# Turned queries and first keys emptied from PSUM for both heads at once, their halves laid out by transfers on ScalarE's queue

## The chip, the cores and the metric

The program runs on one core of a Trainium2 chip, in one launch. The metric is device time in microseconds, lower is better. One core has TensorE (PE, matmul; it writes to PSUM, and only VectorE and ScalarE read PSUM here), VectorE (DVE), ScalarE (ACT), GpSimd (POOL) and SyncE (SP), each with an instruction queue of its own that is worked off in order. Transfers are issued from the queues of SP, ACT or POOL and are moved by 16 DMA engines.

## The reference

Two layers; each is a SwiGLU feed-forward half step, a mixer, and another feed-forward half step, over 512 positions of width 1024 in fp32. The change lies in the mixer:

```python
def hybrid_mixer(h, ...):
    proj = h @ w_in
    qa, ka, va, ub, qc, kc, vc, f_lin, g_lin = jnp.split(proj, SPLIT_POINTS, axis=-1)
    ya = chunked_relpos_attention(ha(qa), ha(ka), ha(va), qk_gain[0], qk_gain[1], rel_bias)
    yb = multiscale_pool(ub, w_pool, pool_scale)
    yc = forgetting_attention(hc(qc), hc(kc), hc(vc), qk_gain[2], qk_gain[3], f_lin + forget_bias)
    ys = jnp.stack([ya, yb, yc], axis=2)
    branch = jnp.einsum('bsnw,nwd->bsnd', ys, w_branch)
    gates = jax.nn.sigmoid(g_lin.reshape(B, S, N_BRANCHES, D_MODEL))
    return jnp.sum(gates * branch, axis=2) @ w_out
```

Both attentions have 8 heads of width 64. Queries and keys are RMS-normalised per head and multiplied by a gain (`rms_norm(q, gq) * dh ** -0.5`), logits are `q . k` plus a bias (the first) or a difference of summed forget gates (the second), masked, then softmax and the product with the values.

## The kernel before, in words

**Numbers in two parts.** Every fp32 operand is split into a high part (fp32r) and a low part, the rest, and a product is three matmuls: high x high, high x low, low x high (`triple`, lines L140 to L142 for projections with 512 columns). A weight chunk `raw` is loaded by SP (L303), its high part is made by a cast on ACT (L312) and its low part by a subtraction on DVE (L314).

**The mixer.** `run` projects the first attention's queries (column 0), its keys (1), the forget gates and its values (2), one behind the other. Then come the 8 heads of the first attention ("a"), and between its steps, as filler, the projections of the second attention's queries (column 3), keys (4) and values (5). The second attention ("c") follows. `attention` goes over heads and, in a head, over four blocks of 128 queries. One step is `logits` (two matmuls: for odd and even heads the high and the low part of the query against a key tile that holds high and low), DVE adds the bias and takes the maximum (L1154), ACT takes the exponential (L1158), DVE the reciprocal of the sum (L1160), GpSimd scales (L1162; DVE for the last block). Some units later the weights are transposed on TensorE (L1174), taken out of PSUM in two parts by ACT (L1178) and DVE (L1179), and multiplied with the values (L1196, L1197); ACT and DVE take the result out (L1200 to L1202). After each step the filler yields projections until a budget of TensorE units is used.

**Queries and keys.** `proj_qk` copies a projection out of PSUM (L1001), squares it (ACT L1003), sums the squares (DVE L1004), and forms and applies the norms (DVE, L1022). `turn(p)`, once for each pair of heads (p from 0 to 3), transposes 128 columns (4 instructions, L1027) into a PSUM tile `pt` of 128 x 512: the even head's 64 numbers in the upper 64 partitions, the odd head's in the lower. It then fills tiles `b` of 128 x 2 x 512. A key tile holds, for each head, the high part on the head's own partitions and the low part on the other ones. A query of the version before has two tiles: the high part on both halves (ACT writes the own half at L1036, a transfer on GpSimd's queue copies it to the other, L1039), and the low part on the own half (DVE, L1042) with zeros on the other (GpSimd, L1040). ACT and DVE do this for the even head, then for the odd one.

**Order of the work.** The PSUM pool behind `mmt()` has four banks; turns, logits, weights' transposes and products with the values share it. Tiles `b` come from a pool of 17, tiles `v2` from one of 4. The order in which work is written out is set by a clock `pe[0]` that counts estimated TensorE time: `later(delay, fn)` gives a task a due time, and `poll()`, called in every product, runs the tasks that are due. `ready(p)` is due `TURN` (52) units and 12 per pair behind the end of a projection, 12 more for the first keys, and waits for a head of the attention to be reached (`Q_GATE`, `K_GATE`). A list scheduler then sets each engine's order. The tile names of the order shown below carry a running number.

Of the kernel before, what the change touches and what calls it, by code (L numbers as in the profile page):

```python
# [15 lines left out]
F32 = mybir.dt.float32  # L16
F32R = mybir.dt.float32r
I32 = mybir.dt.int32
AF = mybir.ActivationFunctionType
ALU = mybir.AluOpType  # L20
AX = mybir.AxisListType

P = 128
# [17 lines left out]
def encoder_kernel(tc, xT, c, w_ada, b_ada, gains, w_gate, w_up, w_down, w_qkv, w_f, w_ubg,  # L41
                   qk_gain, rel, fbias, w_pool, pool_scale, w_branch, w_out, inv_cnt, w_first, out):
    nc = tc.nc
# [12 lines left out]
    mm = nc.tensor.matmul  # L56
# [7 lines left out]
    def st(shape, dt, tag, bufs):  # L64
        return sb.tile(shape, dt, tag=tag, bufs=bufs, name=nm(tag))
# [25 lines left out]
    def mmt(shape=(P, T)):  # L91
        return ps.tile(list(shape), F32, tag="mm", bufs=4, name=nm("mm"))

    def blk(tag, dt=F32R):
        bufs = {"xv": 4, "v2": 4, "b": NB}[tag]
        return st([P, 2, T], dt, tag, bufs)

    def t1(cols=T):
        return st([P, cols], F32, "t1", 2)

    def t2(cols=T):
        return st([P, cols], F32, "t2", 3)
# [16 lines left out]
    def later(delay, fn, group=None):  # L119
        t = Task(pe[0] + delay, fn, group)  # L120
        tasks.append(t)
        return t
# [197 lines left out]
    def rsqrt_steps(v, n):  # L320

        jt = st([P, n], I32, "nt_j", 2)
        nc.vector.tensor_scalar(jt, v.bitcast(I32), -0.5, 1597463007.0, op0=ALU.mult, op1=ALU.add)
        y = jt.bitcast(F32)
        for _ in range(3):
            yield y
            q = st([P, n], F32, "nt_q", 1)
            u = st([P, n], F32, "nt_u", 1)
            z = st([P, n], F32, "nt_z", 2)
            nc.vector.tensor_tensor(q, y, y, op=ALU.mult)  # L330
            nc.vector.scalar_tensor_tensor(u, q, -0.5, v, op0=ALU.mult, op1=ALU.mult)
            nc.vector.scalar_tensor_tensor(z, u, 1.5, y, op0=ALU.add, op1=ALU.mult)
            y = z
        yield y
# [656 lines left out]
        res.extend(vt)  # L991

    def proj_qk(l, col, gcol, is_q, res, pre=None, norm=None):
        lows = []
        qs = []

        def evac(t, a):
            if t == 0:
                qs.extend((st([P, NT, T], F32, "ptb", 2), st([P, NT, H], F32, "qss", 1)))
            qn, ss = qs  # L1000
            nc.scalar.copy(qn[:, t, :], a)  # L1001
            sq = t2(T)
            nc.scalar.activation(sq, qn[:, t, :], AF.Square)  # L1003
            nc.vector.tensor_reduce(ss[:, t, :], sq.rearrange("p (h d) -> p h d", h=H), axis=AX.X, op=ALU.add)  # L1004

        yield from proj(l, col, evac, pre, norm)
        qn, ss = qs
        norm_of = {}

        def first():  # L1010
            v = st([P, NT * H], F32, "nt_v32", 2)
            nc.vector.tensor_scalar(v, ss.rearrange("p t h -> p (t h)"), 1.0 / HD, EPS, op0=ALU.mult, op1=ALU.add)
            norm_of["steps"] = rsqrt_steps(v, NT * H)
            next(norm_of["steps"])

        def step():
            norm_of["r"] = next(norm_of["steps"])

        def scale(t):
            q3 = qn[:, t, :].rearrange("p (h d) -> p h d", h=H)  # L1020
            r = norm_of["r"][:, t * H:(t + 1) * H].unsqueeze(2).to_broadcast([P, H, HD])
            nc.vector.tensor_tensor(q3, q3, r, op=ALU.mult)  # L1022

        def turn(p):
            pt = mmt()
            for t in range(NT):
                nc.tensor.transpose(pt[:, t * P:(t + 1) * P], qn[:, t, p * P:(p + 1) * P], ident)  # L1027
            pe[0] += 2.2
            b = blk("b")
            if is_q:  # L1030
                lows.append(blk("b"))
            first, second = slice(0, HD), slice(HD, P)
            for odd, (own, other) in enumerate(((first, second), (second, first))):
                dst = b[:, odd, :]
                gc = gcol[own, :]
                nc.scalar.activation(dst[own, :], pt[own, :], AF.Identity, scale=gc)  # L1036
                low = dst[other, :]
                if is_q:
                    nc.gpsimd.dma_start(low.bitcast(F32), dst[own, :].bitcast(F32))  # L1039
                    nc.gpsimd.memset(lows[p][other, odd, :].bitcast(F32), 0.0)  # L1040
                    low = lows[p][own, odd, :]
                nc.vector.scalar_tensor_tensor(low, pt[own, :], gc, dst[own, :].bitcast(F32),  # L1042
                                               op0=ALU.mult, op1=ALU.subtract)
            res.append((b, lows[p]) if is_q else b)

        todo = [first, step, step, step] + [lambda t=t: scale(t) for t in range(NT)]
        todo += [lambda p=p: turn(p) for p in range(4)]
        turns.append(todo)
        for n in range(8):
            later(PACE * n, lambda n=n: todo.pop(0)() if len(todo) == 12 - n else None)  # L1050

        def ready(p):
            if len(todo) >= 4 - p:
                if heads[0] < (Q_GATE if is_q else K_GATE)[p]:
                    later(8, lambda: ready(p))
                else:
                    while len(todo) >= 4 - p:
                        todo.pop(0)()

        for p in range(4):  # L1060
            later(TURN + (12 if col == 1 else 0) + 12 * p, lambda p=p: ready(p))

    turns = []
    heads = [2 * H]
    TURN = 52
# [73 lines left out]
    def attention(qs, ks, vs, strip, ys, filler, budget, group):  # L1139
# [3 lines left out]

        def logits(h, i, strips):
            p, off = divmod(h, 2)
            (q, ql), k = qs[p], ks[p]
            odd = h % 2
            n = (i + 1) * P
            s = mmt()
            mm(s[:, :n], q[:, odd, i * P:(i + 1) * P], k[:, odd, :n], start=True, stop=False)  # L1150
            mm(s[:, :n], ql[:, odd, i * P:(i + 1) * P], k[:, odd, :n], start=False, stop=True)
            lg = t1(T)[:, :n]
            mx = st([P, 1], F32, "mx", 4)
            nc.vector.tensor_tensor_reduce(out=lg, in0=s[:, :n], in1=strips[i], scale=-1.0, scalar=BIG,  # L1154
                                           op0=ALU.add, op1=ALU.min, accum_out=mx)
            pr = t2(T)[:, :n]
            sm = st([P, 1], F32, "sm", 4)
            nc.scalar.activation(pr, lg, AF.Exp, bias=mx, scale=-1.0, accum_out=sm)  # L1158
            rs = st([P, 1], F32, "rs", 4)
            nc.vector.reciprocal(rs, sm)  # L1160
            eng = nc.vector if i == NT - 1 else nc.gpsimd
            eng.tensor_scalar(pr, pr, rs, None, op0=ALU.mult)  # L1162
            pe[0] += 0.5 * (i + 1.5)
            later(LAG_T, lambda: turn(h, i, pr), group)
# [446 lines left out]
```

## Time and profile before

| | |
|---|---|
| median of 3 runs | 2321.46 us (2320.78 to 2321.69) |
| profiled execution | 2320.73 us, span 2318.9 us, TensorE clock 1.0 |
| TensorE (PE) busy | 2296.4 us, 99% of the span |
| VectorE (DVE) busy | 1848.0 us, 80% |
| ScalarE (ACT) busy | 1242.5 us, 54% |
| GpSimd (POOL) busy | 277.1 us, 12% |
| DMA | 325.26 MB, 140 GB/s mean |
| first queries' and keys' turns, first layer | about 398 to 436 us |
| first attention, first layer | from about 437 us; turns of the second attention's queries from 481 us |

The profile shows one execution. "Busy" of an engine is the time in which it had an instruction; "a <- b" in a list of waits says that the engine sat idle before a until b was done. A row of a group gives line, engine, operation, tiles, count, then busy us, mean ns of one, and the idle time of the engine ahead of it with what ended it. A row of a window gives its bounds, its length, the busy time of PE, PEld, DVE, ACT and POOL with their counts, the clock, the DMA share and GB/s. The chain lists, in order of time, the work that ended last. A queue with a q behind it (SPq, ACTq) is the engine's sequencer, which issues transfers.

### The profile page before, as it was taken

The page shows a single profiled execution, that of the slowest core. Times are in us where ns is not written, and L with a number is a line of the kernel's source. Part 1 is how long each engine was busy: PE and PEld are TensorE (multiplying, and loading weights), DVE is VectorE, ACT ScalarE, POOL GpSimd, SP SyncE. Part 2 cuts the span into 40 slices and gives each one's busy share as a digit, 9 for nine tenths or more (in the row PEclk, how much of TensorE's full clock was granted, in tenths as well). Part 3 has the DMA queues.
Part 4 walks back from the last instruction along what each step waited for, and adds up shares of the span by engine and source line. Part 5 has one row for each costly group of instructions (what it writes and reads, how often), then busy time and mean ns, then how long its engine had stood idle before and what let it go on. Part 6 is the DMA issues. An engine that isn't in the chain of part 4 may idle for free.

```text
span 2318.9 us, 38895 instructions
## 1 busy us (share of the span) xinstructions
PE 2296.4 (99%) x14826; PEld 2067.5 (89%) x14826; DVE 1848.0 (80%) x3205; ACT 1242.5 (54%) x2252; POOL 277.1 (12%) x413
## 2 busy tenths in 40 slices
PE   7999999999999999999999999999999999999999
PEld 5898998878889898989999989988788898999898
DVE  8988886787698678888788989777877995859593
ACT  5363555677645463635463636466765554636362
POOL 2000011244400000000000000112443001000000
PEclk9999999999999999999999999999999999999999
DMA  8736353333334526373526372533332445133332
GB/s 300 256 101 243 121 192 99 106 97 116 104 114 146 191 73 218 96 259 101 190 74 218 92 271 93 200 109 101 94 119 94 122 152 172 55 118 97 114 92 100
DMA packets 142174, 325.26 MB, mean 140 GB/s; under 512 B 14338, under 2 KB 16514, under 8 KB 141988
## 3 DMA queue, kind: packets, MB, share of 16 engines
q1 hardware_dynamic: 137426, 307.57, 40.9%
q0 software_dynamic: 4560, 15.21, 2.1%
q8 instruction: 116, 1.90, 0.3%
q14 instruction: 70, 0.57, 0.1%
q10 hardware_dynamic: 2, 0.00, 0.0%
HBM read 312.16 MB, written 6.38 MB: 137 GB/s over the span
## 4 chain that ended last, share of the span: by engine, by line
PE 93%; DVE 3%; ACT 2%; issue 1%; DMA 0%; SPq 0%; POOL 0%; ACTq 0%; DVEq 0%
PE acc L140 13%; PE acc L142 13%; PE acc L141 13%; PE acc L149 7%; PE acc L151 7%; PE acc L150 7%; PE mm L151 5%; PE mm L149 5%; PE mm L150 5%; PE mm L140 5%; PE mm L141 5%; PE mm L142 4%; PE mm L1174 1%; PE mm L1197 1%; PE mm L1196 1%
## 5 line engine op out<-in xcount | busy, mean ns | idle before, releaser
L312 ACT CAST w<-raw 128x1024 fp32r<-128x1024 f32 x205 | 212.8, 1047 | 226.2 <-PE acc L142 142.8
L140 PE MATMUL acc<-b,w 128*128 128x512 f32 (+1 forms) x880 | 326.6, 371 | 0.0
L141 PE MATMUL acc<-b,w 128*128 128x512 f32 (+1 forms) x880 | 323.3, 367 | 0.0
L142 PE MATMUL acc<-b,w 128*128 128x512 f32 (+1 forms) x880 | 323.2, 367 | 0.0
L314 DVE TENSOR_TENSOR w<-raw,w 128x1024 fp32r<-128x1024 f32 x205 | 248.6, 1223 | 88.7 <-ACT w L312 85.1
L142 PEld LDWEIGHTS acc<-b,w 128*128 128x128 f32 x880 | 165.4, 188 | 28.0
L140 PEld LDWEIGHTS acc<-b,w 128*128 128x128 f32 x880 | 165.4, 188 | 26.2
L141 PEld LDWEIGHTS acc<-b,w 128*128 128x128 f32 x880 | 165.4, 188 | 25.9
L149 PE MATMUL acc<-b,ptb 128*128 128x256 f32 x588 | 162.8, 277 | 0.0
L150 PE MATMUL acc<-b,ptb 128*128 128x256 f32 x588 | 162.7, 277 | 0.0
L151 PE MATMUL acc<-b,ptb 128*128 128x256 f32 x588 | 162.6, 277 | 0.0
L140 PE MATMUL acc<-w,hhi 128*128 128x512 f32 x336 | 138.3, 412 | 0.0
L142 PE MATMUL acc<-w,hlo 128*128 128x512 f32 x336 | 131.8, 392 | 0.0
L141 PE MATMUL acc<-w,hhi 128*128 128x512 f32 x336 | 131.7, 392 | 0.0
L565 DVE TENSOR_TENSOR ptb<-pta,ptb 128x1024 fp32r<-128x1024 f32 x70 | 85.7, 1224 | 50.9 <-ACT ptb L564 49.8
L473 DVE SCALAR_TENSOR_TENSOR xv<-acc,badac,xv 128x512 f32<-128x512 f32 (+1 forms) x112 | 77.2, 690 | 58.7 <-PE acc L142 58.7
L149 PE MATMUL mm<-b,ptb 128*128 128x256 f32 x420 | 115.9, 276 | 0.0
L150 PE MATMUL mm<-b,ptb 128*128 128x256 f32 x420 | 115.9, 276 | 0.0
L151 PE MATMUL mm<-b,ptb 128*128 128x256 f32 x420 | 115.9, 276 | 0.0
L565 DVE TENSOR_TENSOR w<-v,w 128x1024 fp32r<-128x1024 f32 x84 | 102.5, 1220 | 16.8 <-ACT w L564 16.8
L226 DVE CUSTOM_DVE_ANT_0 v<-v,b,badac 128x1024 f32<-128x1024 f32 x90 | 113.7, 1278 | 1.9 <-DMA v<-in_w_ada_dram 1.8
L564 ACT CAST w<-v 128x1024 fp32r<-128x1024 f32 x84 | 87.8, 1046 | 42.9 <-PE acc L142 31.5
(346 smaller groups left out, 7368.2 us busy)
## 6 DMA issues: line engine op xcount, KB each, us to landing
v<-in_w_ada_dram SPq DMA_DIRECT2D x106, 512.0 KB, 5.4
raw<-in_w_down_dram SPq DMA_DIRECT2D x88, 512.0 KB, 4.5
raw<-in_w_qkv_dram SPq DMA_DIRECT2D x42, 512.0 KB, 3.6
v<-in_w_gate_dram SPq DMA_DIRECT2D x70, 256.0 KB, 3.5
v<-in_w_up_dram SPq DMA_DIRECT2D x70, 256.0 KB, 3.9
raw<-in_w_gate_dram SPq DMA_DIRECT2D x70, 256.0 KB, 7.2
raw<-in_w_up_dram SPq DMA_DIRECT2D x70, 256.0 KB, 3.4
raw<-in_w_ubg_dram SPq DMA_DIRECT2D x28, 512.0 KB, 3.6
```

The lines of the kernel that those rows point to most:

```text
L140: mm(o, lh, rh, start=start, stop=False)
L141: mm(o, lh, rl, start=False, stop=False)
L142: mm(o, ll, rh, start=False, stop=stop)
L149: mm(o, lh, rh, start=start and k == 0, stop=False, skip_group_check=True)
L150: mm(o, lh, rl, start=False, stop=False, skip_group_check=True)
L151: mm(o, ll, rh, start=False, stop=k == 3, skip_group_check=True)
L226: product = lambda: nc.vector.tensor_tensor_reduce(out=raw, in0=raw, in1=silc[0], scale=1.0, scalar=badac[:, l, j, d:d + 1], op0=ALU.mult, ...
L312: nc.scalar.copy(hi, raw)
L314: lo_eng.tensor_tensor(lo, raw, hi.bitcast(F32), op=ALU.subtract)
L473: nc.vector.scalar_tensor_tensor(x, acc_j, gate, x, op0=ALU.mult, op1=ALU.add)
L564: act_(lambda: nc.scalar.copy(pair[0], src))
L565: vec_(lambda: nc.vector.tensor_tensor(pair[1], src, pair[0].bitcast(F32), op=ALU.subtract))
```

## The change

For the first queries, the first keys and the second queries (columns 0, 1 and 3) a turn takes the whole PSUM tile out with one ACT instruction (high part, both heads, 128 x 512) and one DVE instruction (low part) into a tile `both` of the pool `v2`. Four transfers on ACT's queue lay the halves out. A query pair has now one tile per head, high part on both halves of the partitions in plane 0, low part on both halves in plane 1 (four transfers of 64 x 1024); a key tile keeps its layout (four of 64 x 512). GpSimd's transfers and zeros are gone. The second keys (column 4) keep the old way. The logits' two matmuls read the query's planes 0 and 1. Turns of columns 3 and 4 are due 8 units later.

```diff
             b = blk("b")
-            if is_q:
-                lows.append(blk("b"))
             first, second = slice(0, HD), slice(HD, P)
-            for odd, (own, other) in enumerate(((first, second), (second, first))):
-                dst = b[:, odd, :]
-                gc = gcol[own, :]
-                nc.scalar.activation(dst[own, :], pt[own, :], AF.Identity, scale=gc)
-                low = dst[other, :]
+            if col in (0, 1, 3):
+                both = blk("v2")
+                nc.scalar.activation(both[:, 0, :], pt, AF.Identity, scale=gcol)
+                nc.vector.scalar_tensor_tensor(both[:, 1, :], pt, gcol, both[:, 0, :].bitcast(F32),
+                                               op0=ALU.mult, op1=ALU.subtract)
                 if is_q:
-                    nc.gpsimd.dma_start(low.bitcast(F32), dst[own, :].bitcast(F32))
-                    nc.gpsimd.memset(lows[p][other, odd, :].bitcast(F32), 0.0)
-                    low = lows[p][own, odd, :]
-                nc.vector.scalar_tensor_tensor(low, pt[own, :], gc, dst[own, :].bitcast(F32),
-                                               op0=ALU.mult, op1=ALU.subtract)
-            res.append((b, lows[p]) if is_q else b)
+                    c = blk("b")
+                    moves = [(o[rows], both[own]) for o, own in ((b, first), (c, second)) for rows in (first, second)]
+                else:
+                    moves = [(b[first, 0], both[first, 0]), (b[second, 0], both[first, 1]),
+                             (b[first, 1], both[second, 1]), (b[second, 1], both[second, 0])]
+                for o, part in moves:
+                    nc.scalar.dma_start(o.bitcast(F32), part.bitcast(F32))
+            else:
+                for odd, (own, other) in enumerate(((first, second), (second, first))):
...
+            res.append((b, c) if is_q else b)
...
-            later(TURN + (12 if col == 1 else 0) + 12 * p, lambda p=p: ready(p))
+            later(TURN + (0, 12, 0, 8, 8)[col] + 12 * p, lambda p=p: ready(p))
...
-            (q, ql), k = qs[p], ks[p]
             odd = h % 2
+            q, k = qs[p][odd], ks[p]
...
-            mm(s[:, :n], q[:, odd, i * P:(i + 1) * P], k[:, odd, :n], start=True, stop=False)
-            mm(s[:, :n], ql[:, odd, i * P:(i + 1) * P], k[:, odd, :n], start=False, stop=True)
+            mm(s[:, :n], q[:, 0, i * P:(i + 1) * P], k[:, odd, :n], start=True, stop=False)
+            mm(s[:, :n], q[:, 1, i * P:(i + 1) * P], k[:, odd, :n], start=False, stop=True)
```

Lines of the functions behind it move by some six numbers: the logits are L1150 and L1151 before and L1156 and L1157 now, the exponential L1158 and L1164, the weights' transposes L1174 and L1180, the values' products L1196, L1197 and L1202, L1203; the turn's transposes L1027 and L1026; its ACT instruction L1036 and L1032, its DVE instruction L1042 and L1033, and L1042 is now the transfers.

**What moves on TensorE, at the second attention's queries.** TensorE before, first layer, a little behind the third of these turns; `acc` rows are projections of the second keys (filler), `mm` rows are logits and transposes of the first attention:

```order
L1150 MATMUL mm_5182<-b_4443,b_4195 128x256
L1151 MATMUL mm_5182<-b_4443,b_4196 128x256
L140 MATMUL acc_4864<-w_5160,hhi 128x512
L141 MATMUL acc_4864<-w_5160,hhi 128x512
L142 MATMUL acc_4864<-w_5160,hlo 128x512
L1174 MATMUL mm_5203<-ident,t_851_5083 128x128 x4
L140 MATMUL acc_4865<-w_5155,hhi 128x512
L141 MATMUL acc_4865<-w_5155,hhi 128x512
L142 MATMUL acc_4865<-w_5155,hlo 128x512
```

TensorE now, at the end of the second keys' projection: the rows of `acc_4875` are the end of that filler, and what follows is a product with the values (`mm_5246`) and logits (`mm_5260`), and, behind the rows shown, the fourth query turn and more of attention:

```order
L141 MATMUL acc_4875<-w_5151,hhi 128x512
L142 MATMUL acc_4875<-w_5151,hlo 128x512
L1202 MATMUL mm_5246<-ptb_5124,xv_4413 128x256
L1156 MATMUL mm_5260<-b_4445,b_4193 128x512
L1157 MATMUL mm_5260<-b_4445,b_4193 128x512
L1203 MATMUL mm_5246<-ptb_5124,xv_4413 128x256
L1202 MATMUL mm_5246<-ptb_5124,xv_4456 128x256
L1203 MATMUL mm_5246<-ptb_5124,xv_4456 128x256
L1202 MATMUL mm_5246<-ptb_5124,xv_4486 128x256
L1203 MATMUL mm_5246<-ptb_5124,xv_4486 128x256
L1202 MATMUL mm_5246<-ptb_5124,xv_4508 128x128
```

Before, three to six projections stand between two steps of attention. Now the projections of the second keys stand in long rows (18, then 25 in a row) ahead of this place, and from `mm_5246` on 44 instructions of attention and turns follow without a projection between them; the next projection reads `w_5397`. The longest such row before has 14 instructions.

**On ACT, in the same place.** ACT before, from the first query turn to the third; `w_5372` is the same weight chunk as `w_5397` now:

```order
L1036 ACTIVATE b_5050<-mm_5045,qg_110 64x512 x2
L1200 COPY yl_5072<-mm_5063 64x256
L1036 ACTIVATE b_5094<-mm_5089,qg_110 64x512
L1202 CAST b_4971<-yl_5072 64x256
L1178 CAST pta_5040<-mm_5104 128x2x128
L1158 ACTIVATE t_851_5083,sm_5084<-t_849_5080,mx_5081 128x512
L1036 ACTIVATE b_5094<-mm_5089,qg_110 64x512
L312 CAST w_5372<-raw_5370 128x1024
L1036 ACTIVATE b_5123<-mm_5118,qg_110 64x512
L1178 CAST ptb_5133<-mm_5134 128x3x128
L1158 ACTIVATE t_866_5147,sm_5148<-t_864_5144,mx_5145 128x128
L1200 COPY yl_5171<-mm_5166 64x256
```

ACT now, from the fourth query turn's last transfers to the cast of that chunk:

```order
L1042 DMA b_5281<-v_915_5278 64x1024 x2
L1002 ACTIVATE t_918_5292<-ptb_5202 128x512
L1164 ACTIVATE t_922_5311,sm_5312<-t_920_5308,mx_5309 128x128
L1002 ACTIVATE t_925_5321<-ptb_5202 128x512
L1184 CAST ptb_5324<-mm_5325 128x3x128
L1206 COPY yl_5337<-mm_5332 64x256
L1164 ACTIVATE t_934_5351,sm_5352<-t_932_5348,mx_5349 128x256
L1184 CAST ptb_5324<-mm_5366 128x4x128
L1164 ACTIVATE t_942_5381,sm_5382<-t_940_5378,mx_5379 128x384
L1208 CAST b_5331<-yl_5337 64x256
L1000 COPY ptb_5202<-acc_4875 128x512
L312 CAST w_5397<-raw_5395 128x1024
```

The cast of the next chunk, which stood between the second and the third query turn, now stands behind all four turns and their 16 transfers, and behind the copies and squares of the second keys (L1000, L1002).

**On ACT, at the first keys.** ACT before, from the second key turn (L1036) to the first exponential of attention; `xv` rows are copies of the values out of PSUM (L986):

```order
L1036 ACTIVATE b_4424<-mm_4419,qkgc 64x512
L1036 ACTIVATE b_4443<-mm_4438,qkgc 64x512
L986 CAST xv_4451<-acc_4311 128x4x64
L1036 ACTIVATE b_4443<-mm_4438,qkgc 64x512
L986 CAST xv_4451<-acc_4311 128x4x64
L1036 ACTIVATE b_4467<-mm_4462,qkgc 64x512
L986 CAST xv_4478<-acc_4312 128x4x64
L1036 ACTIVATE b_4467<-mm_4462,qkgc 64x512
L986 CAST xv_4478<-acc_4312 128x4x64
L986 CAST xv_4500<-acc_4313 128x4x64 x2
L1158 ACT_TABLE_LOAD
L1158 ACTIVATE t_685_4514,sm_4515<-t_683_4511,mx_4512 128x128
```

ACT now, from the second key tile's transfers to that exponential:

```order
L1042 DMA b_4423<-v_677_4424 64x512 x4
L1032 ACTIVATE v_680_4446<-mm_4440,qkgc 128x512
L986 CAST xv_4456<-acc_4307 128x4x64
L1042 DMA b_4445<-v_680_4446 64x512 x4
L986 CAST xv_4456<-acc_4307 128x4x64
L1032 ACTIVATE v_684_4473<-mm_4467,qkgc 128x512
L986 CAST xv_4486<-acc_4308 128x4x64
L1042 DMA b_4472<-v_684_4473 64x512 x4
L986 CAST xv_4486<-acc_4308 128x4x64
L986 CAST xv_4508<-acc_4309 128x4x64
L1164 ACT_TABLE_LOAD
L1164 ACTIVATE t_693_4522,sm_4523<-t_691_4519,mx_4520 128x128
```

The four transfers of each key tile stand between the copies of the values, and the table load and the first exponential stand behind the last of them.

More of the change, by code (lines that the diff above doesn't have):

```diff
@@ L993, in proj_qk @@
     def proj_qk(l, col, gcol, is_q, res, pre=None, norm=None):
-        lows = []
         qs = []
@@ L1029, in turn @@
             b = blk("b")
-            if is_q:
-                lows.append(blk("b"))
             first, second = slice(0, HD), slice(HD, P)
-            for odd, (own, other) in enumerate(((first, second), (second, first))):
-                dst = b[:, odd, :]
-                gc = gcol[own, :]
-                nc.scalar.activation(dst[own, :], pt[own, :], AF.Identity, scale=gc)
-                low = dst[other, :]
-                if is_q:
-                    nc.gpsimd.dma_start(low.bitcast(F32), dst[own, :].bitcast(F32))
-                    nc.gpsimd.memset(lows[p][other, odd, :].bitcast(F32), 0.0)
-                    low = lows[p][own, odd, :]
-                nc.vector.scalar_tensor_tensor(low, pt[own, :], gc, dst[own, :].bitcast(F32),
-                                               op0=ALU.mult, op1=ALU.subtract)
-            res.append((b, lows[p]) if is_q else b)
+            if col in (0, 1, 3):
[3 more added lines that the diff above has]
+                                               op0=ALU.mult, op1=ALU.subtract)
+                if is_q:
+                    c = blk("b")
[7 more added lines that the diff above has]
+                for odd, (own, other) in enumerate(((first, second), (second, first))):
+                    dst = b[:, odd, :]
+                    gc = gcol[own, :]
+                    nc.scalar.activation(dst[own, :], pt[own, :], AF.Identity, scale=gc)
+                    nc.vector.scalar_tensor_tensor(dst[other, :], pt[own, :], gc, dst[own, :].bitcast(F32),
+                                                   op0=ALU.mult, op1=ALU.subtract)
+            res.append((b, c) if is_q else b)
         todo = [first, step, step, step] + [lambda t=t: scale(t) for t in range(NT)]
```

## The prediction

> **What bounds the kernel now.** I read the page's busy shares and its chain, then TensorE's list of waits, then the chain, the windows and the timeline of the two attentions, where the change lies.
>
> ```profile
> PE   2296.4 (99%) x14826; PEld 2067.5 (89%) x14826; DVE 1848.0 (80%) x3205; ACT 1242.5 (54%) x2252; POOL 277.1 (12%) x413
> PE 93%; DVE 3%; ACT 2%; issue 1%; DMA 0%; SPq 0%; POOL 0%; ACTq 0%; DVEq 0%
> ```
>
> TensorE is the bound: it is busy in 2296.4 of 2318.9 us. The change adds and removes no matmul, so it can move the time only through TensorE's waits. Those of the mixers are these (us in total, times, longest; both layers):
>
> ```profile
> PE mm L1174 <- DVE b L1042: 2.7, 3, 1.2
> PE mm L1027 <- DVE mx L1154: 1.5, 2, 0.8
> PE mm L1197 <- DVE ptb L1179: 0.7, 2, 0.4
> PE mm L1027 <- DVE ptb L1022: 0.6, 2, 0.3
> PE mm L1196 <- ACT ptb L1178: 0.5, 2, 0.3
> PE mm L1027 <- DVE pta L1179: 0.5, 2, 0.2
> ```
>
> Together 6.5 us, and 5.3 of them (the L1174 row and the three of L1027) stand at a turn or right behind one. That is all a better turn can win. The windows say where: 2.4 us per layer of TensorE's idle time lie in the 38 us in which the second attention's queries are turned (38.00 less 35.61, and less 35.33 in the second layer), none in the 16 us in which the first keys are turned.
>
> ```profile
> 424.00:440.00 16.00, 16.00 (x80) 13.27 (x79) 10.99 (x20) 11.30 (x21) 0.62 (x4) 1.00 0.34 100
> 478.00:516.00 38.00, 35.61 (x197) 29.02 (x195) 32.36 (x82) 28.47 (x65) 20.40 (x33) 1.00 0.38 105
> 1625.00:1663.00 38.00, 35.33 (x195) 28.75 (x193) 32.33 (x83) 28.20 (x64) 20.21 (x33) 1.00 0.37 105
> ```
>
> The chain through the longest wait (start us, us, what): the PSUM tile of one turn is emptied by two ACT and two DVE instructions one behind the other, and TensorE's next transposes, which need that bank, start at 483.88.
>
> ```profile
> 481.50 0.75 DVE b L1042
> 482.27 0.69 ACT b L1036
> 482.98 0.77 DVE b L1042
> 483.75 0.14 issue
> 483.88 0.41 PE mm L1174 x2
> ```
>
> **The change, part by part.** Rows for the prices: an ACT and a DVE half (64x512), the transfer that GpSimd issues now with its landing time, SyncE's issue of a weight load, and the one transfer that ACT issues today.
>
> ```profile
> L1036 ACT ACTIVATE b<-mm,qg 64x512 fp32r<-64x512 f32 x16 | 10.9, 684 | 1.9 <-DVE b L1042 0.8 <-PE mm L1027 0.7
> L1042 DVE SCALAR_TENSOR_TENSOR b<-mm,qg,b x32: 737/748/759, 398.9 to 1649.3; 64x512 fp32r<-64x512 f32 x32
> L1039 POOL DMA_DIRECT2D b<-b x32: 516/523/578, 399.1 to 1649.6; - x32
> DMA to landing us min/median/max: 2.1/2.4/5.5
> L303 SPq DMA_DIRECT2D raw<-in_w_qkv_dram x42: 367/368/379, 346.5 to 1652.5; - x42
> L162 ACTq DMA_DIRECT2D b<-in_c_dram x1: 518/518/518, 0.7 to 0.7; - x1
> ```
>
> *Emptying both heads at once.* 24 turns (three kinds, four each, two layers) lose one ACT and one DVE instruction: 16.4 us and 18.0 us. I price the 128x512 forms like the halves, by columns; they read the same 512 (other 128x512 ACT rows below are at 581 to 627 ns). The bank of a turn comes free after one ACT and one DVE instruction, 1.4 us instead of 3.0. What this can return on the path is at most the 5.3 us above.
>
> *GpSimd's transfers and zeroing.* 32 issues and 32 memsets leave a queue that is 12% busy and that no row of TensorE's waits names: 0. At the least it helps nobody, at the most it lets GpSimd's scaling of the weights (L1162) start sooner, which the ACT and DVE rows ahead of it hide.
>
> *The transfers on ACT's queue.* Four per turn, 96 in all. Their price D on ACT is not in the trace; the nearest rows are SyncE's 0.37 us, from 42 loads, and ACT's own single 0.52. The lower end is 0, if an issue lies under the activation that still runs. I take 0.37, the row with many instances and the same 64 to 128 rows of a tile. So ACT gains 35.3 us and loses 16.4. The Trainium skill, DMA: Bandwidth & Descriptors, section "Issuing engines are not separate DMA queues", calls the issue time usually small beside the transfer; here 0.37 stands beside a landing time of 2.4, and if one drew from it that D counts for nothing, ACT's sum below would fall to 18.2 us and the change would be the first or second rival. Against the change speaks the Trainium skill, Perfetto Trace Analysis, section "DMA Instruction — HWDGE (DVE, Sync)": the time shown for a transfer's issue is one in which the sequencer is taken, and the descriptor block is locked for one issuer at a time. By that the full 0.37 falls on ACT, and waits for SyncE's issues on top; no row of this trace shows two issuers meeting.
>
> The bytes rise from 4 MB (32 x 128 KB) to 20 (64 x 256 KB and 32 x 128 KB), of 325 MB, in windows whose DMA share is 0.34 to 0.38: 0. The second attention's queries are read tens of us later. The first keys are the tight ones: two activations and four issues behind 427.6 (below) the first key tile's transfers are out, at 430.5, and by the row above they land between 432.6 and 436.0, while the first logits start at 436.6: 0, though the slow end comes near. An ACT wait for another transfer's landing (issues share a few semaphores) I price at 0, since the ones waited for were issued more than 2.4 us before.
>
> *The new order at the second attention's queries (the main term).* TensorE's program now has the projections of the second keys run out early: 44 instructions of attention stand without one projection between them, where the longest such row was 14. The next projection waits for the cast of w_5397, which is on ACT's queue behind all four query turns with their 16 transfers. I compare the two queues from the first query's activation to that cast, 50 ACT rows:
>
> ```profile
> L1158 ACT ACTIVATE t<-t,mx 128x128 f32<-128x128 f32 (+3 forms) x39 | 21.8, 559 | 14.5 <-DVE mx L1154 12.9 <-DVE v L987 0.8 <-DVE nt_j L323 0.4
> L312 ACT CAST w<-raw 128x1024 fp32r<-128x1024 f32 x20 | 20.8, 1045 | 4.6 <-PE acc L142 3.6 <-DMA raw<-in_w_qkv_dram 0.9
> L1178 ACT CAST ptb<-mm 128x384 fp32r<-128x384 f32 (+1 forms) x18 | 9.5, 527 | 0.4
> L1003 ACT ACTIVATE t<-ptb 128x512 f32<-128x512 f32 x12 | 7.5, 627 | 0.1
> L1202 ACT CAST b<-yl 64x256 fp32r<-64x256 f32 x17 | 6.9, 404 | 7.4 <-DVE yl L1201 7.3
> L1001 ACT COPY ptb<-acc 128x512 f32<-128x512 f32 x12 | 6.9, 581 | 2.4 <-PE acc L142 1.8 <-PE mm L1197 0.6
> L1200 ACT COPY yl<-mm 64x256 f32<-64x256 f32 x17 | 6.2, 368 | 0.9 <-PE mm L1197 0.6
> L1178 ACT CAST pta<-mm 128x128 fp32r<-128x128 f32 (+1 forms) x19 | 5.9, 310 | 2.4 <-PE mm L1174 2.2
> L986 ACT CAST xv<-acc 128x256 fp32r<-128x256 f32 x8 | 3.0, 370 | 1.8 <-PE acc L142 1.0 <-DVE xv L987 0.7
> ```
>
> ACT: 4 turns x 0.684, 8 exponentials x 0.559, 4 casts x 0.527 and 3 x 0.310, 4 casts x 0.404, 3 copies x 0.368, 4 copies x 0.581, 3 squares x 0.627, one cast of 1.045: 18.2 us. With 16 x 0.37 it is 24.1.
>
> TensorE's pace is read from its timeline (start us, us, what): five projections from 484.37 to 485.51 are 0.228 us each, four transposes from 481.55 to 481.96 0.10 each.
>
> ```profile
> 481.55 0.66 PE L1027 MATMUL mm<-ident,ptb 128*128 128x128 f32 x4 [0.23 <-DVE pta L1179]
> 481.96 0.48 PE L140 MATMUL acc<-w,hhi 128*128 128x512 f32 x1
> ...
> 484.37 0.40 PE L140 MATMUL acc<-w,hhi 128*128 128x512 f32 x1
> ...
> 485.51 0.39 PE L142 MATMUL acc<-w,hlo 128*128 128x512 f32 x1
> ```
>
> In the same stretch it has 57 projections (13.0 us), 11,264 columns of logits and weighted values (5.0 at 0.228 per 512) and 32 transposes (3.2): 21.2 us. So ACT is behind by 2.9 us even if it never waits. The other end: in 478 to 516 ACT was busy 28.47 of 38 us, the rest it waited for others; at that share 24.1 us take 32.2, and TensorE waits 11.0. A walk through the rows gave about 9, whose last part is the 44 instructions, where TensorE, ACT and DVE answer each other in turn. I take the middle, 7.0, since neither end is nearer: ACT works ahead under the long rows of projections, and then it doesn't. Off go the 2.4 us of idle time that the window has now: +4.6 us per layer, with ends of +0.5 and +8.6.
>
> *The first keys.* ACT's order there is: two activations, four transfers, a copy, four transfers and so on, up to the first exponential. The rows of today (start us, us, what):
>
> ```profile
> 436.62 0.37 ACT L986 CAST xv<-acc 128x256 fp32r<-128x256 f32 x1 [0.86 <-PE acc L142]
> 437.88 1.28 ACT L1158 ACT_TABLE_LOAD   x1
> 439.17 0.40 ACT L1158 ACTIVATE t<-t,mx 128x128 f32<-128x128 f32 x1
> 439.97 0.61 POOL L1162 TENSOR_SCALAR t<-t,rs 128x128 f32<-128x128 f32 x1 [9.62 <-DVE rs L1160]
> ```
>
> TensorE ends the values' projection at 436.6. After the second key turn it has 36 projections and 8 transposes to do, 9.0 us, so that turn ends at 427.6. From there ACT has 4 x 0.68 + 6 x 0.37 + 16 x 0.37 = 10.9 us, then the table: the first exponential starts at 439.8, against 439.17. Its weights are ready for TensorE 1.4 us later (439.17 to 440.58 today), at 441.2, and TensorE wants them at 436.6 plus 18 projections and three logits, 441.4. So load alone costs 0. The other end: the fourth key's second transfer waits for its low part, which now stands on DVE behind the first two logits' rows, so ACT, which would issue it at 436.6, can stand still for some 2.5 us (two logits, their evictions, the low part) with the copies of the values, the table and the exponentials behind it; TensorE then waits for the weights (441.2 + 2.5 - 441.4 = 2.3) and some 0.9 for the values' copies, 3.2 in all. I take 0.8, nearer to 0, because the window has 4.7 us of ACT idle and the change adds 16 x 0.37 - 4 x 0.68 = 3.2.
>
> *First queries.* ACT has room; the casts of the values' weights move some 4 us later, and are wanted later still: 0, at most one cast's 1.05 if that cover is gone.
>
> *Sum.* (4.6 + 0.8) x 2 = +10.8 us on the profiled 2320.73: 2331.5. The median of the runs lies 0.73 above that execution: 2332.3, I say 2332.
>
> **The rivals.**
>
> *Faster: the bank decides.* A turn's bank is free 1.6 us sooner, ACT's issues lie under its activations (D near 0), and the 5.3 us at turns go: 2316. For it: all of today's long waits are at turns. Against it: the 44 instructions without a projection. It needs ACT's delay under 2.4 us per layer; with ACT never waiting that point is D = (21.2 + 2.4 - 18.2) / 16 = 0.34, and to pass the bound of 4.64 us D has to be below some 0.2.
>
> *No change.* D is about 0.3, ACT works ahead under the 45 projections ahead of the gap, and the new waits are about as long as the old: 2321, within 4.64 us (0.2%, about what runs of this kernel can tell from no change).
>
> *Slower still.* D is ACT's own 0.52: the load is 26.5 us, the ends 5.3 and 14.1, the middle 9.7, less 2.4; and the first keys cost their 3.2: 10.5 x 2 = 21 us, 2342.
>
> **How the numbers follow.** The forecast has 0.48, slower still 0.12, no change 0.2, faster 0.2. Slower by over 0.2% is 0.6, within it 0.2, faster 0.2. The forecast's own range is 2322 to 2343, from (0.5 + 0) x 2 to (8.6 + 1.6) x 2, with half of the keys' upper end. The range given leaves out the better half of the faster case and the worse half of the slowest: 2315 to 2344.
>
> **What would show it.** Right: rows of transfers on ACT near 0.37 us each; ACT's busy share over 56% with them; the row of L1174 waiting for a turn gone; in its place, some 16 us behind the first of the second attention's query turns, one or two gaps of TensorE of 2 us and more, put down to ACT or DVE in attention's transposes or to the cast of the next weights. The window there would have 5 to 9 us of TensorE idle instead of 2.4. Wrong: transfers of 0.1 us or less, or a cast of the next weights that is done before TensorE gets there; or waits for a landing at the first logits, which I priced at 0; or TensorE slower beside the 16 MB of added traffic, which nothing here shows.

## The result, and the profile after

The changed kernel takes 2353.58 us (2352.62 to 2354.6, 4 runs) against 2321.12 us (2320.22 to 2321.69) of the kernel before beside it: ratio 1.014, 95% interval 1.0128 to 1.0152. That is 32 us slower, outside the range that was given, on the side that was forecast, and three times the size.

The profile's first part, the new transfer queue (packets, MB, share of 16 engines) and the chain:

```profile
PE 2308.9 (98%) x14826; PEld 2074.9 (88%) x14826; DVE 1826.0 (78%) x3181; ACT 1223.0 (52%) x2228; POOL 245.2 (10%) x349
...
q10 hardware_dynamic: 7682, 20.98, 3.6%
...
PE 93%; DVE 2%; ACT 2%; ACTq 1%; DMA 1%; issue 1%; POOL 0%; SPq 0%; DVEq 0%; POOLq 0%
```

VectorE lost 22 us of work, ScalarE 20 and GpSimd 32, as the change says: none of it was on the path. ACT's busy share *fell*, because issuing is not counted as busy; it stands under ACTq, which is on the chain now. TensorE's busy time rose by 12.5 us with the same 14826 matmuls; a lowered clock, shown below, accounts for a part of that. Its waits (us, times, longest; lines as in the changed kernel, both layers):

```profile
PE mm L1180 <- POOL t L1168: 11.9, 6, 2.7
PE mm L1026 <- DVE ptb L1021: 4.2, 2, 2.1
PE acc L140 <- ACT w L312: 3.7, 2, 2.1
PE acc L140 <- DVE xv L987: 3.4, 2, 1.7
PE acc L141 <- DVE w L314: 1.1, 2, 0.6
PE mm L1156 <- PE mm L1180: 1.1, 2, 0.5
```

The row that led before, L1174 waiting for a turn's VectorE part, is gone: 25 us of new waits stand against some 6 of old ones. Behind most of this stands one queue. The transfers on ACT's queue (min, median, max in ns; then the time to landing):

```profile
L1042 ACTq DMA_DIRECT2D b<-v x96: 467/608/1985, 398.8 to 1678.7; - x96
DMA to landing us min/median/max: 2.2/4.1/7.0
```

The 96 issues held ACT for 70.1 us in all, 0.73 each. The first of a turn's four takes about 0.47 us and the next two 0.61 mostly; the fourth of a query's takes 1.2 in the median of 16 and up to 2.0. A key's, of half the size, never took over 0.72. In the mean a query's issue held ACT for 0.82 us and a key's for 0.55. Where these issues stood, in three places of each layer:

*At the first queries.* ACT's timeline, and TensorE's below it (start us, us, what):

```profile
413.81 2.98 ACTq L1042 DMA_DIRECT2D b<-v  x4
416.83 0.63 ACT L1002 ACTIVATE t<-ptb 128x512 f32<-128x512 f32 x1 [2.85 <-issue]
417.49 0.58 ACT L1095 COPY t<-mm 8x512 f32<-8x512 f32 x1
417.97 1.99 ACT L312 CAST w<-raw 128x1024 fp32r<-128x1024 f32 x2
...
419.06 1.20 PE L140 MATMUL acc<-w,hhi 128*128 128x512 f32 x4 [1.60 <-ACT w L312]
...
429.09 0.30 PE L1026 MATMUL mm<-ident,ptb 128*128 128x128 f32 x1 [2.09 <-DVE ptb L1021]
```

Behind the last query's four issues stand the forget gates (L1095; in the kernel before L1089, at 412.89) and two casts of the values' weights. In the kernel before, ACT ran these two casts ahead of the gates:

```profile
408.52 1.04 ACT L312 CAST w<-raw 128x1024 fp32r<-128x1024 f32 x1
411.31 1.03 ACT L312 CAST w<-raw 128x1024 fp32r<-128x1024 f32 x1
```

They moved by 9.5 and about 7.6 us and come 1.6 us too late for TensorE. The gates' chain on VectorE comes late too, and the scaling of the first keys (L1021) stands behind it there: 2.09 us at 427.

*At the first keys.* The fourth key's issues and the values' last copies on ACT, the fourth key's low part on VectorE (from the chain), and TensorE's wait for a copy of the values:

```profile
442.84 3.86 ACTq L1042 DMA_DIRECT2D b<-v  x4
446.74 0.65 ACT L986 CAST xv<-acc 128x256 fp32r<-128x256 f32 x2 [3.67 <-issue]
...
444.25 0.66 DVE v L1033
...
447.72 0.47 PE L140 MATMUL acc<-w,hhi 128*128 128x512 f32 x1 [1.69 <-DVE xv L987]
```

Of the 3.86 us, 1.6 are not issuing: the first of the four ends at 443.3, and the second starts at 444.94, when the low part is done.

*At the second queries.* The 44 instructions without a projection begin at 506.9. TensorE waits twice for softmax weights that GpSimd scales, behind exponentials that are late on ACT; for the second, the fourth turn's four issues stand ahead of the exponential:

```profile
512.74 0.90 PE L1180 MATMUL mm<-ident,t 128*128 128x128 f32 x3 [2.71 <-POOL t L1168]
...
513.50 3.04 ACTq L1042 DMA_DIRECT2D b<-v  x4
516.59 0.63 ACT L1002 ACTIVATE t<-ptb 128x512 f32<-128x512 f32 x1 [2.67 <-issue]
...
518.84 0.47 PE L1180 MATMUL mm<-ident,t 128*128 128x128 f32 x1 [2.41 <-POOL t L1168]
```

For the first, the exponential's input was ready at 501.84, 7.8 us before it ran. Ahead of it in ACT's order stood the third turn's four issues (502.86 to 505.88) and a copy of a projection (L1000). VectorE's row, then ACT's, then GpSimd's, and last what the same copy waits for in the second layer:

```profile
501.28 0.56 DVE L1160 CUSTOM_DVE_ANT_0 t<-mm,strip 128x384 f32<-128x384 f32 x1 [0.82 <-PE mm L1157]
508.44 0.59 ACT L1000 COPY ptb<-acc 128x512 f32<-128x512 f32 x1 [5.44 <-DMA b<-v]
...
509.62 0.61 ACT L1164 ACTIVATE t<-t,mx 128x384 f32<-128x384 f32 x1
511.13 0.14 POOL L1125 MEMSET strip<- 64x64 f32 x1 [7.11 <-DMA strip<-in_rel_dram]
ACT ptb L1000 <- PE mm L1203: 5.8, 1, 5.8
```

In the first layer the profile puts the copy's wait down to the landing of a transfer, but the product with the values that it also waits for (L1203, 508.13 and 0.28 us long) ends only 0.02 us earlier, and in the second layer it is that product. The product stands behind the 25 projections on TensorE. So, by these rows, the last 2.5 us of ACT's idle time here, from 505.9 to 508.4, come from the order and not from the issues. GpSimd adds up to 0.7 us: its scaling starts at 511.26, behind a memset that waited for a load, while the reciprocal it needs was done at 510.5.

And TensorE itself slows down there. Windows of 2 us (bounds, length, TensorE's busy time with count, granted clock, DMA share, GB/s):

```profile
508.00:510.00 2.00, 1.46 (x12) 1.00 0.50 115
510.00:512.00 2.00, 0.03 (x1) 0.86 0.21 78
512.00:514.00 2.00, 1.26 (x6) 0.50 0.00 0
...
522.00:524.00 2.00, 2.00 (x7) 0.50 0.46 131
524.00:526.00 2.00, 2.00 (x9) 0.73 0.59 148
526.00:528.00 2.00, 2.00 (x11) 1.00 0.62 179
```

Within the wait from 510 to 512.7 the granted clock falls to 0.50 (0.86 in the mean of 510 to 512: some 1.4 us into the wait, with another half us of waiting just ahead of it), and it stays there for nearly 14 us. At 429.5, behind the wait at 427, it falls as well, for 3.4 us; behind the shorter wait at 446 it does not. The Trainium skill, TensorE: Matmul & The Clock Gate, section "What's actually happening", has half rate follow an idle window of about 3.4 us; this trace agrees with the half rate, but TensorE had idled less than that when the clock fell.

### The profile page after: what moved, and what is told of

Read it like the earlier page. It is cut to its first block, busy times and chain, and to the rows that moved or that the text cites. A ratio compares the mean times of both kernels' runs of the same rounds, so it can differ in the third digit from the quotient of the medians.

```text
span 2352.4 us, 38865 instructions
## 1 busy us (share of the span) xinstructions
PE 2308.9 (98%) x14826; PEld 2074.9 (88%) x14826; DVE 1826.0 (78%) x3181; ACT 1223.0 (52%) x2228; POOL 245.2 (10%) x349
## 4 chain that ended last, share of the span: by engine, by line
PE 93%; DVE 2%; ACT 2%; ACTq 1%; DMA 1%; issue 1%; POOL 0%; SPq 0%; DVEq 0%; POOLq 0%
PE acc L140 13%; PE acc L141 13%; PE acc L142 13%; PE acc L149 7%; PE acc L151 7%; PE acc L150 7%; PE mm L150 5%; PE mm L149 5%; PE mm L151 5%; PE mm L140 4%; PE mm L141 4%; PE mm L142 4%; PE mm L1180 1%; ACTq L1042 1%; PE mm L1203 1%; PE mm L1156 1%
## 5 line engine op out<-in xcount | busy, mean ns | idle before, releaser
L149 PEld LDWEIGHTS acc<-b,ptb 128*128 128x128 f32 x588 | 110.5, 188 | 0.5 <-ACT v L1334 0.4
```

The lines of the kernel that those rows point to most:

```text
L149: mm(o, lh, rh, start=start and k == 0, stop=False, skip_group_check=True)
```

## The experiments

All times are medians, each beside the kernel before on the same chip (2320.6 to 2321.2 us). "The longest stretch" is the longest row of TensorE instructions without a projection near the second queries. Three theories. S: ACT's queue stands still during an issue, and what stands behind is late. O: the new order costs by itself (the due times, the long stretch without projections). T: the 17 MB of added traffic slow the loads. A rival, P, belongs to runs that issue from another queue: what stands behind the issues there is late in its turn.

**The due times taken back, all else as changed.**

```diff
-            later(TURN + (0, 12, 0, 8, 8)[col] + 12 * p, lambda p=p: ready(p))
+            later(TURN + (0, 12, 0, 0, 0)[col] + 12 * p, lambda p=p: ready(p))
```

> The change with the due times of the kernel before (the turns of the second queries and keys no longer 8 units later); TensorE's longest stretch without a projection is then 19 instructions instead of 44. Theory S (ScalarE's queue stands still during its issues, about 0.6 us each, and everything behind it is late): the losses at the first queries (some 6 us per layer) and first keys (some 3) stay, and of the 7 at the second queries about half, since their 16 issues are still there: 2344 to 2349. Theory O (the new order, above all the 44 instructions, is what costs): the second queries lose nothing any more, 2336 to 2341.

2341.4 us, ratio 1.0089 (1.0074 to 1.0104). 12 us come back, and no window shows a lowered clock. About 10 of the 12 are won at the second queries. The rest is won ahead of them: from the first query turn to the table load of the first exponential it takes 49.0 and 48.9 us in the two layers, against 50.8 and 49.6 in the full change and 40.4 in the kernel before. The time lies just above O's range and below S's; the other 20 us stay.

**The transfers on SyncE's queue.**

```diff
-                    nc.scalar.dma_start(o.bitcast(F32), part.bitcast(F32))
+                    nc.sync.dma_start(o.bitcast(F32), part.bitcast(F32))
```

> The change with the same transfers on SyncE's queue instead of ScalarE's; bytes and count are the same. Theory S: nearly all of the 32 us comes back, 2319 to 2326. Theory T (the 17 MB of added traffic slow the weight loads): it stays at 2340 or more. Rival P (SyncE's weight loads now stand behind transfers that wait for ScalarE and VectorE, and come late): 2326 to 2338, with TensorE waiting for casts that wait for loads.

2328.28 us, ratio 1.0034 (1.002 to 1.0048), above S's range and in P's: 25 of 32 us come back with bytes and count the same, so T is out as the main cause. An issue takes SyncE as long as ACT (75.1 us for the 96, 0.78 in the mean), and what TensorE waits for is now a cast whose load stood behind such transfers (rival P). At the first queries nothing is lost any more: the first key turn starts 26.1 us behind the first query turn, as in the kernel before (32.4 in the full change). SyncE's issues:

```profile
L1042 SPq DMA_DIRECT2D b<-v x96: 461/596/1965, 399.1 to 1655.8; - x96
```

The largest of TensorE's waits in its mixers:

```profile
PE acc L140 <- ACT w L312: 5.7, 4, 2.6
```

The order at the second queries changed with it (the longest stretch is 16 instructions), so this run does not separate S from O there.

**One place at a time.** `turn` takes the new way only for the columns named, `if col in (3,)` for the second queries, `(0,)` for the first, `(1,)` for the first keys; the others go the old way. New due times in all three.

> Only the second queries in the new way (first queries and keys as before, GpSimd's transfers and zeros for them); due times as in the change, and the stretch of 44 is there. If the losses of the three places add up: 2321 plus 2 x 7, 2335 (2331 to 2339). If the waits at the second queries come from the delay carried over from the first ones (theory C), this is 2321 to 2326.

> Only the first queries in the new way, the rest as before but for the due times. If the losses add up: 2321 plus 2 x 6, 2333 (2330 to 2336), with the same three waits for a cast, a low part and the scaled keys at 417 to 429 us. If the issues at the first queries are hidden when the keys' ones are gone: 2321 to 2325.

> Only the first keys in the new way, queries as before; new due times. If the three places add up: 2353.6 - 2336.8 - 2330.6 + 2 x 2321.2, so 2328.6 (2326 to 2331), with the waits for the values' copies (1.7), and for GpSimd's scaled weights (1.0), per layer. If the keys cost only because the first queries made ScalarE late: 2320 to 2323.

2336.84, 2330.59 and 2323.49 us (ratios 1.0067, 1.004 and 1.0011). The first two lie in the ranges of "the losses add up"; the third lies between its two ranges and in neither. All three forecasts count from 2321, which the next run puts right.

**Nothing but the new due times, in the kernel before.**

```diff
-            later(TURN + (12 if col == 1 else 0) + 12 * p, lambda p=p: ready(p))
+            later(TURN + (0, 12, 0, 8, 8)[col] + 12 * p, lambda p=p: ready(p))
```

> The kernel before with nothing but the new due times (turns of the second queries and keys 8 units later). Theory S (issues on ScalarE's queue cost, the order only through what stands behind them): 2318 to 2324, no change. Theory O (the order by itself costs): 2327 to 2334, since the version with the old due times was 12 us under the full change.

2318.19 us, ratio 0.9989 (0.9979 to 0.9998): 2.9 us *faster*. The new due times by themselves help. Counted from here, the three places cost 18.6 (second queries), 12.4 (first queries) and 5.3 us (first keys): 36.3, and the full change stands 35.4 above this kernel. The losses add up to within 1 us, so none of them is in the main a delay carried over from another place. The first queries alone show the same two waits as above, here 3.3 and 2.5 us for the two layers together:

```profile
PE acc L140 <- ACT w L312: 3.3, 2, 1.7
PE mm L1026 <- DVE ptb L1021: 2.5, 2, 2.1
```

**The transfers on GpSimd's queue.** (`nc.gpsimd.dma_start`.)

> The change with the transfers on GpSimd's queue, which is 10% busy. Theory S: 2318 to 2326. Rival P (the queue that issues makes late what stands behind it, here GpSimd's scaling of the softmax weights and its share of the results): 2328 to 2338, with TensorE waiting for L1168 on GpSimd.

2325.2 us, ratio 1.0017 (1.0008 to 1.0027). At the upper edge of S, and the wait it leaves is P's:

```profile
PE mm L1180 <- POOL t L1168: 3.6, 4, 1.0
```

The order changed here too (the longest stretch is 18 instructions), so this run does not separate S from O at the second queries either.

**Twice the issues, the same bytes.**

```diff
+                if is_q:
+                    moves = [(o[:, i], part[:, i]) for o, part in moves for i in range(2)]
                 for o, part in moves:
```

> The change with each of the queries' transfers cut in two (64x512 instead of 64x1024): the same bytes, 64 more issues, all on ScalarE. If an issue has a price of its own (0.5 to 0.6 us): 38 us more work on ScalarE at the places that are late now, 2365 to 2385. If the price goes by the bytes that the queue has to take: each takes about half, 2350 to 2357.

2378.3 us, in a single run, and in the range of "a price of its own". The 160 issues:

```profile
L1044 ACTq DMA_DIRECT2D b<-v x160: 468/607/1722, 398.1 to 1705.6; - x160
```

The median is the same. The mean falls from 0.73 to 0.59 us, and that of a query's issue from 0.82 to 0.60, because long issues become rare: 3 of 128 take over 0.9 us, where it was 21 of 64. So the price goes mostly by the issue, and the tail by the size. All issues together hold ACT for 94.6 us, 24.5 more than in the full change, and the kernel takes 24.7 us longer. That the two agree so closely does not show a price of one to one: the longest stretch is 16 instructions here and not 44, so the order is another one.

**The second queries with the old due times.** (Only column 3 in the new way, due times `(0, 12, 0, 0, 0)`.)

> Only the second queries in the new way, with the due times of the kernel before: the same 32 issues on ScalarE as with the new due times, but TensorE's longest stretch without a projection is 19 instructions, not 44. If the issues cost by their load on ScalarE alone: 2333 to 2338, as with the new due times (2336.8). If they cost only where the order leaves no projections beside them: 2321 to 2327.

2324.83 us, ratio 1.0018 (1.0008 to 1.0028). With the runs above this makes a square:

| second queries | old due times | new due times |
|---|---|---|
| old way | 2321.1 | 2318.2 |
| new way, 32 issues on ACT | 2324.8 | 2336.8 |

The issues alone cost 4, the due times alone gain 3, and together they cost 16. Neither S nor O by itself gives that. But the stretch of 44 stands in the last cell alone (the longest is 19 with the old due times in the new way, and 16 with the new ones in the old way), so the square cannot tell the stretch from the issues in it. The windows from 478 to 516 us, with the old due times and then with the new ones (bounds, length, busy time of PE, PEld, DVE, ACT and POOL with counts, clock, DMA share, GB/s):

```profile
478.00:516.00 38.00, 35.32 (x184) 28.43 (x184) 22.70 (x60) 21.66 (x54) 10.67 (x15) 1.00 0.65 167
```

```profile
478.00:516.00 38.00, 31.49 (x157) 25.94 (x156) 21.73 (x61) 21.00 (x53) 11.63 (x16) 0.84 0.56 146
```

With the stretch of 44, TensorE idles 3.8 us longer in the window, does 27 matmuls fewer, and at a lower clock. How the cost divides between the stretch and the issues inside it needs further runs.

**One turn's transfers moved to SyncE.** Second queries alone, new due times; `nc.sync` for the fourth turn (`p == 3`) in one kernel, for the third (`p == 2`) in the other. Both leave 12 of 16 issues per layer on ACT.

> Only the second queries in the new way, new due times, and the fourth turn's four transfers on SyncE's queue. The long stretch without a projection stays (48 instructions), and of the 16 issues per layer the four that lie inside it leave ScalarE (3.0 us of its time there). If the stretch costs by ScalarE's issues inside it: some 3 us less per layer than with all on ScalarE (2336.8), with less time at half clock besides, 2326 to 2332. If the stretch costs by its order alone: 2333 to 2338.

> Only the second queries in the new way, new due times, and the third turn's four transfers on SyncE's queue instead of the fourth's: as many issues left on ScalarE, but the longest stretch without a projection is 18 instructions. If the order decides: 2319 to 2325. If the number of issues on ScalarE decides: the same as with the fourth turn's moved, within 2 us.

2332.02 us (1.0043, 1.0028 to 1.0058) with the long stretch, at the top of its first range; 2325.52 (1.0017, 1.0007 to 1.0027) without it, half a microsecond above the range for "the order decides". Of the 18.6 us that the new way costs here with the new due times, the four issues inside the stretch are 4.8; with as many issues on ACT, the version with the stretch is 6.5 slower. Without the stretch the 12 issues per layer that are left still cost 7.3 us against the kernel with the new due times alone (2318.19). With the fourth turn's issues gone, the second wait for GpSimd's weights is no longer in the list and the first stays at 2.7 us, once per layer, as it should if the copy of the projection holds it up:

```profile
PE mm L1190 <- POOL t L1178: 5.4, 2, 2.7
```

No run has the long stretch and no issue on ACT, so what the order costs by itself stays open.

**Versions without an issue on ACT, and a later due time.** Second queries alone, on SyncE; first keys alone, on SyncE; and the kernel before with the second queries' turns 16 units later instead of 8 (`(0, 12, 0, 16, 8)`).

> Only the second queries in the new way, new due times, their transfers on SyncE's queue. ScalarE then has no issue and the stretch of 44 is not there: 2315 to 2321, at or under the version with nothing but the new due times (2318.2). If the issues make the weight loads late that stand behind them on SyncE: 2322 to 2328.

> Only the first keys in the new way, new due times, transfers on SyncE's queue. With them on ScalarE it was 2323.5. If those 5 us were ScalarE's issues: 2316 to 2320. If SyncE's weight loads come late there (in the version with all transfers on SyncE TensorE waits 2.7 us for a cast at 437 us): 2321 to 2326.

> The kernel before with the second queries' turns 16 units later and the second keys' 8. If the gain of the new due times (2.9 us) comes from turns that no longer meet the end of an attention step's transposes, another 8 units give about as much or nothing: 2314 to 2319. If it was the luck of one place: 2318 to 2323.

2318.45 us (0.9991, 0.9982 to 1.0), 2318.14 (0.9989, 0.998 to 0.9998) and 2319.35 (0.9995, 0.9985 to 1.0004). Without issues on ACT the new way is neither dearer nor cheaper than the old: both stand within 0.3 us of the kernel with nothing but the due times. (The first queries were not run alone on SyncE.) Emptying a bank in 1.4 us instead of 3.0 gains nothing once the turn comes 8 units later; that alone had already taken the longest wait for a turn away. Another 8 units give no more; that time lies in the range of "the luck of one place", so what the first 8 units gain by is not shown. Among the versions at 2318 the simplest is the kernel before with the new due times, which beats both kernels.

## Why the prediction was right and wrong, point by point

**TensorE as the bound, its waits as the only lever, a gain of 6.5 us at most.** The bound is right: VectorE, ScalarE and GpSimd lost 20 to 32 us of work each, and the kernel became slower. So is the limit: the best version gains 2.9. "Only through TensorE's waits" is wrong: of the 33.5 us between the two profiles 21.0 are idle time of TensorE and 12.5 busy time, with the same matmuls.

**Emptying both heads at once.** The price was right: 0.690 us for the ACT and 0.749 for the VectorE form, as the halves. The old wait at the bank did go.

**The transfers' price D: the term that was mis-sized.** Taken at 0.37 us from SyncE's weight loads, with 0.52 as the upper end; measured 0.73 in the mean (70.1 us / 96), 0.61 in the median, beyond the upper end. The step that failed is the choice of the nearest row: a load of a weight chunk on SyncE is not nearer to a transfer of 64 partitions within the chip's own memory than ACT's single issue was. It was not a matter of the engine: on SyncE the same transfers take 0.60 in the median, 0.78 in the mean. And it had a tail, the fourth issue of a turn at 1.2 us and more, which a single D leaves out.

**Transfers landing.** Right nearly throughout: TensorE never waits for one of these transfers, at the first logits or elsewhere. ACT's list names a landing twice, 2.2 us ahead of a turn and the 5.4 us ahead of the copy at 508.44, where the product with the values ended as late. That the issue holds its queue is shown by ACT's rows: 2.98, 3.86 and 3.04 us of issuing between two of its instructions, with 1.6 us for the low part in the second. The Trainium skill, Perfetto Trace Analysis, section "DMA Instruction — HWDGE (DVE, Sync)", says as much of the time shown for an issue, and the trace agrees.

**The second queries.** The mechanism was right, place, long stretch and late ACT included. The working gave +4.6 us per layer with ends of 0.5 and 8.6; the runs show 7.8 against the kernel before (15.7 / 2) when only this place is changed, within the ends. With the issues as measured in the full change (12.9 us for 16) the load end of the same sum is 18.2 + 12.9 - 21.2 = 9.9, less 2.4: 7.5. ACT's rows bear this out: from the first turn's activation to the end of that cast it took 32.1 us (490.24 to 522.32), against 31.1 in the sum. So D accounts for most of the miss here. But what the sum calls waiting was not all waiting. In the profile of the version with this place alone TensorE's busy time is

```profile
PE 2305.1 (99%) x14826; PEld 2075.2 (89%) x14826; DVE 1841.8 (79%) x3197; ACT 1236.3 (53%) x2244; POOL 262.0 (11%) x381
```

8.7 us more than the 2296.4 before, and its idle time only 7.0 more. The runs add what the sum did not say: it is the order and the issues together.

**The first keys.** Taken 0.8, with an end of 3.2 for the fourth key's transfer that waits for its low part. Measured 5.3 / 2 = 2.7 per layer, with the waits that the upper end named, and the wait for the low part is there (1.6 us). The choice "nearer to 0" failed: a key's issue took 0.55 us and not 0.37, and the low part did hold ACT up.

**The first queries: the second step that failed.** Priced at 0, at most one cast's 1.05. They cost 12.4 / 2 = 6.2 us per layer. This is the only one of the three places that fell outside the ends given to it, and it alone takes the time out of the range: 2353.6 less 12.4 is about 2341 (an estimate from the runs of single places). The forecast had the casts move "some 4 us"; they moved 9.5 and 7.6, because the 16 issues there took 13.7 us (3.83 + 3.03 + 3.90 + 2.98) and not 5.9. So the cover was lost through D. And I had looked at when the casts' result is wanted and not at the forget gates, which stand behind the same issues and have VectorE's scaling of the keys behind them.

**A cost that was not on the list: the clock.** From 512 to 525 us TensorE was busy for about 9.5 us at half clock, so up to 4.7 us per layer are owed to it there, and up to 1.7 at 430, in the first layer only. Not all of the 12.5 us by which TensorE's busy time grew can be put down to it: in the version with the old due times the clock stayed at 1.00, and the busy time (2303.7) is still 7.3 us longer than before. What that part is stays open. No run separates the clock from the waits that bring it about.

**The rivals.** "Faster" needed ACT never late, and fell. "Slower still" had the right cause, D, and the wrong ceiling, since it kept the first queries at 0 and had no clock. (The upper end of the forecast's own range comes to 2342 by its sum, not 2343.)

## What to carry to other kernels

Price a transfer's issue by a row of the same kind (both ends on chip, as many partitions, as many of them back to back), and when there is none, let the range reach far beyond the nearest one. Issues belong to a queue that nothing urgent stands behind: list, for each, what follows on that engine until the next slack, and follow it through other engines' queues too. Before an elaborate edit, try the part of it that costs nothing: here eight units of a due time gave 2.9 us, and no version gave more.

## What the runs showed of the hardware that I had not expected

- Most issues of a transfer within the chip's memory held the issuing queue for 0.47 to 0.61 us; the median was 0.61 on ScalarE's queue, 0.60 on SyncE's and 0.52 on GpSimd's, and 0.61 for 128 KB as for 256 KB.
- Of four such issues of 256 KB in a row on ScalarE, the fourth took 0.6 to 2.0 us. Those of 128 KB for the keys showed no such growth, and on GpSimd's queue none took over 0.73.
- TensorE's clock fell to half some 1.4 us into a wait of 2.7 us and came back only after nearly 14 us, with a further wait of 2.4 us between. At 427 it fell behind a wait of 2.09 us, and in the version with the old due times it did not fall behind one of 2.08 us at the same place, nor in the full change behind one of 1.7 us (446). So the length of a single wait does not decide.
